# First projection of a hybrid layer in token layout, MoBA values 512 wide, and a new order of all engines

## The chip, the cores and the metric

The kernel runs on one core of a Trainium2 chip. The metric is the device time of one execution in microseconds; lower is better. The engines are named as the profile names them: PE is TensorE (matmuls; PEld its weight loads), DVE is VectorE, ACT is ScalarE, POOL is GpSimd, SP is SyncE, which issues the DMAs.

## The reference

One decoder layer on 256 tokens of width 1024, in fp32. One input projection gives the columns of three groups of heads, each group mixes the tokens in its own way and is multiplied by its own gate, and one output projection with a layer norm ends the layer:

```python
h = jnp.einsum('btd,de->bte', x, w_in)            # 256 x 1024 by 1024 x 4176
h_gla, h_moba, h_rwkv = _split(h, [GLA_COLS, MOBA_COLS, RWKV_COLS])
o = jnp.concatenate([_gla_branch(h_gla, ...), _moba_branch(h_moba, ...), _rwkv_branch(h_rwkv, ...)], axis=-1)
y = jnp.einsum('bte,ed->btd', o, w_out)
return _layer_norm(DN_ALPHA * x + y, ln_w, ln_b)
```

GLA (4 heads of 64) is linear attention with a decay for each channel, which comes from 16 low-rank columns. MoBA (8 heads) is causal softmax attention with a bias by relative position; at 256 tokens its one block is the whole sequence. RWKV-7 (4 heads) is a recurrence over the tokens whose state is multiplied by a diagonal and a rank-one term in each step; its decay and its in-context rate come from 64 low-rank columns.

## The kernel before

**Projections.** The columns of `w_in` are cut on the host into 16 units of 256 columns (`starts`, `wun`), and the 80 low-rank columns. x comes transposed, in 8 chunks of 128 input channels, with the columns of unit 0 and the low-rank columns beside it (`xw0`, DMA chunks `xw`). fp32 products are made of three fast matmuls: each operand is split into a high part (`hi`, a copy on ACT that rounds) and a low part (`lo`, a subtraction on DVE), and hi x hi, hi x lo and lo x hi are added up in PSUM (`terms`). So a unit costs a DMA of 1 MB into a `raw` tile, two `hi` copies on ACT, two `lo` subtractions on DVE (`prep`), and 48 matmuls of 256 columns on PE: 8 chunks x 3 terms x 2 halves. In channel layout (`proj_ch`) the weights are the stationary operand and x is streamed; in token layout (`proj_tok`) x is stationary and the weights are streamed. Groups of 6 matmuls (`GRAIN`) stay together.

**The first group** needs no `raw` tile, since its weights come with x: unit 0, the RWKV keys (`pk`, two PSUM tiles of 256 columns), and the low-rank columns (`pg`, 80 rows). For each chunk, ACT and DVE split x (256 columns), unit 0 (256) and the low-rank part (80); the first chunk is multiplied in plain fp32 without a split. Eight matmuls on a constant (`warm`) stand at its head.

**Mixers.** RWKV builds a 128 x 128 matrix `AT` for each pair of heads, solves triangular systems of 32 rows with DVE (`pre`, `T`, 31 steps), transposes the result (`TT`), and goes on from there through `pX`, `X`, `pP`, `U`, `M`, `yr` to `orw`. MoBA makes scores `pL` of heads 0 to 3 and 4 to 7 from split queries and keys, adds the bias `nB` and takes the row maximum in one DVE instruction for each piece (256 and 128 columns), and exponentiates on ACT (`L`), scales by `rc`, transposes (`pPm`, `PT`), and multiplies by the values `mv` (`pO`, `omb`). Each branch's output is split once more (`ohr`, `ohg`, `ohm`: high parts for RWKV, GLA and MoBA) for the output projection `yo`, whose weights (`rawo`) ACT centres and splits. PSUM has two pools of four banks, `pj` (projections, half of the scores, `yo`) and `sm` (the rest). SBUF tiles of the tag `big` (3 buffers) hold `AT`, `nB`, `xres` and `lwb` one after another.

**Order.** Every instruction is only recorded (`Plan`, `Proxy`); `emit`, whose line is L369 in the profile, then issues the 958 recorded operations in the order of the table `ORDER`, and each engine runs its own in that order. So the place of an instruction is a matter of the table, and all lines of the profile say L369; tiles tell the instructions apart.

## Time and profile before

| | us |
|---|---|
| median of 3 runs | 170.37 |
| lowest and highest | 168.59, 172.09 |
| the profiled execution | 168.87 |
| its span, first to last instruction | 167.2 |
| PE, DVE, ACT, POOL busy | 156.0, 143.1, 118.6, 29.1 |

The profiled execution's own time is 1.67 us longer than its span; the sum of the prediction is made against 168.87. Busy times overlap, since the engines run side by side; which of them decides changes along the span, and the views of the section below are cut by stretch for that reason.

### The profile page before, as it was taken

The page shows a single profiled execution, that of the slowest core. Times are in us where ns is not written, and L with a number is a line of the kernel's source. Part 1 is how long each engine was busy: PE and PEld are TensorE (multiplying, and loading weights), DVE is VectorE, ACT ScalarE, POOL GpSimd, SP SyncE. Part 2 cuts the span into 40 slices and gives each one's busy share as a digit, 9 for nine tenths or more (in the row PEclk, how much of TensorE's full clock was granted, in tenths as well). Part 3 has the DMA queues.
Part 4 walks back from the last instruction along what each step waited for, and adds up shares of the span by engine and source line. Part 5 has one row for each costly group of instructions (what it writes and reads, how often), then busy time and mean ns, then how long its engine had stood idle before and what let it go on. Part 6 is the DMA issues. An engine that isn't in the chain of part 4 may idle for free.

```text
span 167.2 us, 3968 instructions
## 1 busy us (share of the span) xinstructions
PE 156.0 (93%) x1507; PEld 144.6 (86%) x1507; DVE 143.1 (86%) x339; ACT 118.6 (71%) x270; POOL 29.1 (17%) x65
## 2 busy tenths in 40 slices
PE   8869999999999999999999998998998999999940
PEld 3659999999999999999999998997887977888940
DVE  0696899999899999899999999998964969886892
ACT  3494998979934486598683999969998979930000
POOL 8670008930000000001000000000003580120000
PEclk9999999999999999999999999999999999999995
DMA  5999285498466979772850745796243800000203
GB/s 147 328 363 340 105 277 228 129 360 287 114 216 181 167 269 301 281 257 54 253 195 4 250 145 146 208 328 226 70 185 107 258 18 0 0 0 0 94 36 126
DMA packets 18195, 29.47 MB, mean 176 GB/s; under 512 B 6472, under 2 KB 11040, under 8 KB 18176
## 3 DMA queue, kind: packets, MB, share of 16 engines
q1 hardware_dynamic: 18176, 29.21, 55.4%
q8 instruction: 12, 0.20, 0.4%
q14 instruction: 7, 0.06, 0.1%
HBM read 26.97 MB, written 2.24 MB: 175 GB/s over the span
## 4 chain that ended last, share of the span: by engine, by line
PE 42%; DVE 27%; ACT 11%; DMA 8%; issue 7%; SPq 2%; DVEq 0%; ACTq 0%
PE yo L369 13%; DVE lo L369 9%; DMA nB<-vd 5%; DVE pre L369 4%; PE pgq L369 4%; PE pgk L369 3%; PE pv L369 3%; PE pmk L369 3%; DVE L L369 3%; DMA xw<-in_xw_dram 3%; DVE T L369 3%; ACT rawo L369 3%; PE pmq L369 2%; PE pmg L369 2%; DVE Z L369 2%
## 5 line engine op out<-in xcount | busy, mean ns | idle before, releaser
L369 ACT ACTIVATE hi<-raw 128x1024 fp32r<-128x1024 f32 (+1 forms) x32 | 31.2, 998 | 15.0 <-PE pmv L369 3.1
L369 DVE TENSOR_TENSOR lo<-raw,hi 128x1024 fp32r<-128x1024 f32 (+1 forms) x32 | 36.7, 1158 | 0.6 <-ACT hi L369 0.5
L369 POOL TENSOR_SCALAR suo<-suo 128x1 f32<-128x1 f32 x8 | 2.6, 333 | 85.4 <-ACT rawo L369 85.3
L369 DVE SCALAR_TENSOR_TENSOR loo<-rawo,suo,hio 128x512 fp32r<-128x512 f32 (+1 forms) x12 | 10.9, 922 | 0.4 <-ACT hio L369 0.4
L369 DVE TENSOR_TENSOR pre<-T,A 128x1 f32<-128x1 f32 (+30 forms) x31 | 10.3, 331 | 0.5
L369 ACT ACTIVATE lsd<-lmv,eps 128x1 f32<-128x1 f32 x2 | 0.6, 294 | 13.9 <-DVE lmv L369 13.9
L369 ACT ACTIVATE hio<-rawo,suo 128x512 fp32r<-128x512 f32 (+1 forms) x12 | 9.9, 855 | 0.0
L369 PE MATMUL pmg<-xhi,hi 128*128 128x256 f32 x32 | 9.6, 300 | 0.0
L369 PE MATMUL pmv<-hi,xhi 128*128 128x256 f32 x32 | 9.6, 299 | 0.0
L369 PE MATMUL pmk<-xhi,hi 128*128 128x256 f32 x32 | 9.1, 285 | 0.0
L369 PE MATMUL pmq<-xhi,hi 128*128 128x256 f32 x32 | 9.1, 284 | 0.0
L369 PE MATMUL pmg<-xhi,lo 128*128 128x256 f32 x32 | 9.0, 282 | 0.0
L369 PE MATMUL pmg<-xlo,hi 128*128 128x256 f32 x32 | 9.0, 282 | 0.0
L369 PE MATMUL pmq<-xlo,hi 128*128 128x256 f32 x32 | 9.0, 282 | 0.0
L369 PE MATMUL pmq<-xhi,lo 128*128 128x256 f32 x32 | 9.0, 281 | 0.0
L369 PE MATMUL pmv<-lo,xhi 128*128 128x256 f32 x32 | 9.0, 281 | 0.0
L369 PE MATMUL pmv<-hi,xlo 128*128 128x256 f32 x32 | 9.0, 281 | 0.0
L369 PE MATMUL pmk<-xlo,hi 128*128 128x256 f32 x32 | 9.0, 281 | 0.0
L369 PE MATMUL pmk<-xhi,lo 128*128 128x256 f32 x32 | 9.0, 281 | 0.0
L369 ACT ACTIVATE rawo<-rawo 128x1024 f32<-128x1024 f32 x8 | 8.4, 1054 | 0.0
L369 DVE TENSOR_REDUCE T<-pre 128x1 f32<-128x2 f32 (+30 forms) x31 | 7.9, 254 | 0.4
L369 ACT ACTIVATE L<-L,mx 128x256 f32<-128x256 f32 (+1 forms) x16 | 7.1, 447 | 0.3 <-DVE mx L369 0.3
(352 smaller groups left out, 618.4 us busy)
## 6 DMA issues: line engine op xcount, KB each, us to landing
raw<-in_wun_dram SPq DMA_DIRECT2D x28, 512.0 KB, 4.8
rawo<-in_wo_dram SPq DMA_DIRECT2D x8, 512.0 KB, 4.8
xw<-in_xw_dram SPq DMA_DIRECT2D x8, 296.0 KB, 5.1
raw<-in_wun_dram SPq DMA_DIRECT2D x4, 256.0 KB, 6.0
nB<-vd SPq DMA_DIRECT2D x1, 1024.0 KB, 8.3
xres<-in_xr_dram SPq DMA_DIRECT2D x1, 1024.0 KB, 7.6
out_dram<-y SPq DMA_DIRECT2D x3, 256.0 KB, 2.1
dT<-AT SPq DMA_DIRECT2D x2, 256.0 KB, 6.7
```

Of the source, the lines that this page charges most:

```text
L369: self.tc.keep_in_program_order(fn(*args, **kw))
```

## The change

- **First group.** Unit 0 becomes the GLA values. They and the 80 low-rank columns are projected together in token layout, 336 columns wide, into two PSUM tiles `pgv` (one for each 128 tokens). The splits of unit 0 and of the low-rank part become one of 336 columns (`first`: six chunks in one `big` buffer for high and one for low parts, the last chunk in small tiles). ACT copies the low-rank columns to `g0`, PE transposes them back into channel layout (`pg`), and ACT copies the values to `gv`.
- **Units.** The RWKV keys are now unit 1 with a projection of their own (`kproj`, `pk`), RWKV r is unit 2 (one PSUM tile `pr`), and the RWKV values unit 6. The GLA value projection of before, and its ACT copy, are gone.
- **MoBA values.** Units 8 and 9 are laid out on the host as 4 chunks of 512 columns each, and one projection makes all 512 value columns: 48 matmuls of 512 in groups of 3, into `pmv0` and `pmv1`, which hold a PSUM bank each from the first group of three until four ACT copies of 256 columns.
- **Loads.** All eight x chunks are issued ahead of the parameters and the bias table.
- **Warm matmuls.** Eight as before; seven then one stood at the head of the first group, now two stand there, three within it, and three further on in the stream.
- **Order.** The table has 928 entries, in another order throughout. Among others, scores `pL` 4 to 7 come early as before, `pL` 0 to 3 behind the RWKV solve.

```diff
 KC = 8
 LEVELS = (4, 8, 16, 32)
 ORDER = (
...
-    950, 951, 956, 957, 952, 954, 953, 955)
+    903, 899, 897, 910, 908, 909, 911, 912, 916, 917, 900, 919, 898, 920, 918, 921, 922, 923, 924, 926, 925, 927)
...
-    gp = ctx.enter_context(tc.tile_pool(name="gp", bufs=35))
+    gp = ctx.enter_context(tc.tile_pool(name="gp", bufs=37))
...
-    hi0 = wp.tile([128, KC, T], F32R, tag="hi", name="hi0")
-    lo0 = wp.tile([128, KC, T], F32R, tag="lo", name="lo0")
-    units[0] = (hi0, lo0)
-    g0hi = cp.tile([128, KC, 80], F32R, name="g0hi")
-    g0lo = cp.tile([128, KC, 80], F32R, name="g0lo")
+    first = []
+    for nm in ("h", "l"):
+        most = gp.tile([128, 6, XW - T], F32R, tag="big", bufs=3, name=f"f{nm}")
+        rest = gt(f"f{nm}7", (128, XW - T), F32R)
+        first.append([None] + [most[:, k] for k in range(6)] + [rest])
     with plan.at(-2000):
         for k0, k1 in steps[1:] + steps[:1]:
             k = slice(k0, k1)
             raw = xw[k0 // 4][:, k0 % 4:k0 % 4 + k1 - k0]
             split(xhi[:, k], xlo[:, k], raw[:, :, 0:T])
             if k0:
-                split(hi0[:, k], lo0[:, k], raw[:, :, T:2 * T])
-                split(g0hi[:, k], g0lo[:, k], raw[:, :, 2 * T:XW])
+                split(first[0][k0], first[1][k0], raw[:, 0, T:XW])
...
-    def proj_tok(u, name):
-        p = pj(name)
-        for t in range(2):
-            for n, (k, x, w) in grains(terms(XS, units[u])):
-                PE.matmul(p[:, t * 256:(t + 1) * 256], lhsT=x[:, k, t * 128:(t + 1) * 128], rhs=w[:, k, :],
-                          start=(n == 0), stop=(n == 23))
-        return p
...
-    pk = [pj(f"pk{c}") for c in range(2)]
-    pg = pj("pg0")
+    pgv = [pj(f"pgv{t}") for t in range(2)]
     with plan.at(-1500):
-        for c in range(2):
-            PE.matmul(pk[c][:, 0:256], lhsT=xw[0][:, 0, T + c * 128:T + (c + 1) * 128], rhs=xw[0][:, 0, 0:T], start=True, stop=False)
-        PE.matmul(pg[:80, 0:256], lhsT=xw[0][:, 0, 2 * T:XW], rhs=xw[0][:, 0, 0:T], start=True, stop=False)
-        for n, ((k, w, x), (_, wg, _)) in enumerate(zip(terms(units[0], XS), terms((g0hi, g0lo), XS))):
+        for t in range(2):
+            PE.matmul(pgv[t][:, 0:XW - T], lhsT=xw[0][:, 0, t * 128:(t + 1) * 128], rhs=xw[0][:, 0, T:XW], start=True, stop=False)
+        for n, (k, x, w) in enumerate(terms(XS, first)):
             if k == 0:
                 continue
-            for c in range(2):
-                PE.matmul(pk[c][:, 0:256], lhsT=w[:, k, c * 128:(c + 1) * 128], rhs=x[:, k, :], start=False, stop=(n == 23))
-            PE.matmul(pg[:80, 0:256], lhsT=wg[:, k, :], rhs=x[:, k, :], start=False, stop=(n == 23))
+            for t in range(2):
+                PE.matmul(pgv[t][:, 0:XW - T], lhsT=x[:, k, t * 128:(t + 1) * 128], rhs=w[k], start=False, stop=(n == 23))
+    gv = cp.tile([128, 512], F32, name="gv")
+    g0 = gt("g0", (128, 160))
+    for t in range(2):
+        S.activation(g0[:, t * 80:(t + 1) * 80], pgv[t][:, 256:336], AF.Copy)
+    pg = sm("pg0", (128, 256))
+    transposes([(pg[:80, t * 128:(t + 1) * 128], g0[:, t * 80:(t + 1) * 80]) for t in range(2)])
+    for t in range(2):
+        S.activation(gv[:, t * 256:(t + 1) * 256], pgv[t][:, 0:256], AF.Copy)
+
+
+    plan.section = "kproj"
+    pk = [pj(f"pk{c}") for c in range(2)]
+    for n, (k, w, x) in grains(terms(units[1], XS)):
+        for c in range(2):
+            PE.matmul(pk[c][:, 0:256], lhsT=w[:, k, c * 128:(c + 1) * 128], rhs=x[:, k, :], start=(n == 0), stop=(n == 23))
...
-    pr = [pj("pr0"), sm("pr1")]
-    for n, (k, w, x) in grains(terms(units[1], XS)):
-        for c in range(2):
-            PE.matmul(pr[c][:, 0:256], lhsT=w[:, k, c * 128:(c + 1) * 128], rhs=x[:, k, :], start=(n == 0), stop=(n == 23))
-    rf = shift(pr, 0, "rf")
+    rf = shift(proj_ch(2, "pr"), 0, "rf")
     V.tensor_mul(ar[:, :, 1, :], rf.rearrange("p (a b) -> p a b", b=128), Pf[:, :, 1:129])
 
+    prep(6)
...
-    pv = proj_ch(2, "pv")
+    pv = proj_ch(6, "pv")
...
     prep(8)
+    prep(9)
...
+    def moba_values():
+
+        plan.section = "mv0"
+        ps_ = [pj(f"pmv{t}") for t in range(2)]
+        for q in range(2):
+            wh, wl = (w.rearrange("p (a b) c -> p a (b c)", b=2) for w in units[8 + q])
+            for t in range(2):
+                for k in range(4):
+                    with plan.group():
+                        for n, (x, w) in enumerate(((xhi, wh), (xhi, wl), (xlo, wh))):
+                            PE.matmul(ps_[t], lhsT=x[:, q * 4 + k, t * 128:(t + 1) * 128], rhs=w[:, k, :],
+                                      start=(q == 0 and k == 0 and n == 0), stop=(q == 1 and k == 3 and n == 2))
+        for i in range(2):
+            o = gt(f"mv{i}")
+            for t in range(2):
+                S.activation(o[:, t * 256:(t + 1) * 256], ps_[t][:, i * 256:(i + 1) * 256], AF.Copy)
+            mvt.append(o)
+
     def moba_proj(i):
-        for kind, u, dst in (("v", 8 + i, mvt), ("q", 10 + i, mq), ("k", 12 + i, mk)):
+        if i == 0:
+            moba_values()
+        yield
+        for kind, u, dst in (("q", 10 + i, mq), ("k", 12 + i, mk)):
             plan.section = f"m{kind}{i}"
-            p = proj_tok(u, f"pmv{i}") if kind == "v" else proj_ch(u, f"pm{kind}{i}")
-            if kind == "v":
-                o = gt(f"mv{i}")
-                S.activation(o, p, AF.Copy)
-            else:
-                c = 0.125 if kind == "q" else 1.0
-                hi, lo = gt(f"mh{kind}{i}", dt=F32R), gt(f"ml{kind}{i}", dt=F32R)
-                S.activation(hi, p, AF.Copy, scale=c)
-                V.scalar_tensor_tensor(lo, p, c, hi.bitcast(F32), op0=ALU.mult, op1=ALU.subtract)
-                o = (hi, lo)
-            dst.append(o)
+            p = proj_ch(u, f"pm{kind}{i}")
+            c = 0.125 if kind == "q" else 1.0
+            hi, lo = gt(f"mh{kind}{i}", dt=F32R), gt(f"ml{kind}{i}", dt=F32R)
+            S.activation(hi, p, AF.Copy, scale=c)
+            V.scalar_tensor_tensor(lo, p, c, hi.bitcast(F32), op0=ALU.mult, op1=ALU.subtract)
+            dst.append((hi, lo))
...
-    prep(6)
     next(it)
-    prep(9)
...
-    plan.section = "gv"
-    pvg = proj_tok(6, "pgv")
-    gv = gt("gv")
-    S.activation(gv, pvg, AF.Copy)
...
-    starts = [RW + 256, RW, RW + 512, RW + 768, GL, GL + 256, GL + 512, GL + 768]
+    starts = [GL + 512, RW + 256, RW, RW + 768, GL, GL + 256, RW + 512, GL + 768]
     starts += [MB + 1024, MB + 1280, MB, MB + 256, MB + 512, MB + 768, MB + 1536, MB + 1792]
+    wide = cols(MB + 1024, 512).reshape(128, 2, KC, 256)
+    units = [wide[:, i - 8] if i in (8, 9) else cols(c, 256) for i, c in enumerate(starts)]
...
-        wun=np.stack([cols(s, 256) for s in starts]),
+        wun=np.stack(units),
```

The order moves nearly everything; three places follow. Names are tiles, output left of the arrow, and the numbers are buffer numbers.

PE at its start, before (`xw` is the unsplit first chunk, `xhi` and `xlo` the split x, `hi0` and `g0hi` the split first weights):

```order
L369 MATMUL warm_74<-const-bfloat16-1.0 128x512
L369 MATMUL pk0_105<-xw0_72 128x256
L369 MATMUL pk1_106<-xw0_72 128x256
L369 LDWEIGHTS const-bfloat16-1.0
L369 MATMUL warm_74<-const-bfloat16-1.0 128x512
L369 MATMUL pg0_107<-xw0_72 80x256
L369 MATMUL pg0_107<-xhi_80,g0hi_84 80x256
L369 MATMUL pk1_106<-xhi_80,hi0_82 128x256
L369 MATMUL pk0_105<-xhi_80,hi0_82 128x256
L369 MATMUL pg0_107<-xlo_81,g0hi_84 80x256
L369 MATMUL pg0_107<-xhi_80,g0lo_85 80x256
```

PE at its start, after (`fh` and `fl` are the split first weights of 336 columns):

```order
L367 MATMUL warm_74<-const-bfloat16-1.0 128x512
L367 MATMUL pgv1_106<-xw0_72 128x336
L367 LDWEIGHTS const-bfloat16-1.0
L367 MATMUL warm_74<-const-bfloat16-1.0 128x512
L367 MATMUL pgv0_105<-xw0_72 128x336
L367 MATMUL pgv0_105<-fh_82,xhi_80 128x336
L367 MATMUL pgv0_105<-fl_84,xhi_80 128x336
L367 MATMUL pgv0_105<-fh_82,xlo_81 128x336
L367 MATMUL pgv1_106<-fh_82,xhi_80 128x336
L367 MATMUL pgv1_106<-fl_84,xhi_80 128x336
L367 MATMUL pgv1_106<-fh_82,xlo_81 128x336
```

Three matmuls for each term, with the low-rank ones 80 rows high, become two of 336 columns; of the warm matmuls all but a few are gone from the head.

PE around the scores of heads 4 to 7 (`pL4` to `pL7`), before (`pmk0` is the projection of MoBA keys):

```order
L369 MATMUL pmv0_257<-hi8_217,xhi_80 128x256
L369 MATMUL pmv0_257<-lo8_218,xhi_80 128x256
L369 MATMUL pmv0_257<-hi8_217,xlo_81 128x256
...
L369 MATMUL pL6_344<-mlk1_338,mhq1_331 128x128
L369 MATMUL pL7_345<-mlk1_338,mhq1_331 128x128
L369 MATMUL pmk0_268<-xhi_80,hi12_260 128x256
L369 MATMUL pmk0_268<-xlo_81,hi12_260 128x256
L369 MATMUL pmk0_268<-xhi_80,lo12_261 128x256
```

The same place after (`pv` is the projection of RWKV values):

```order
L367 MATMUL pL6_345<-mlk1_339,mhq1_332 128x128
L367 MATMUL pL7_346<-mlk1_339,mhq1_332 128x128
L367 MATMUL pmv0_266<-hi8_223,xhi_80 128x512
L367 MATMUL pmv0_266<-lo8_224,xhi_80 128x512
L367 MATMUL pmv0_266<-hi8_223,xlo_81 128x512
...
L367 MATMUL pmv1_267<-lo8_224,xhi_80 128x512
L367 MATMUL pmv1_267<-hi8_223,xlo_81 128x512
L367 MATMUL pv_168<-xhi_80,hi6_145 128x256
L367 MATMUL pv_168<-xlo_81,hi6_145 128x256
L367 MATMUL pv_168<-xhi_80,lo6_146 128x256
```

Ahead of the scores one value projection of 48 matmuls was finished, with one PSUM tile; after, 15 of the 512-wide matmuls follow the scores and two value tiles stay open, and the next projection behind them is `pv`.

ACT from the first copy behind the solve (`X`), before:

```order
L369 ACTIVATE gr_373<-pgr_372,der_99 128x256
L369 ACTIVATE L5_352<-L5_352,rc5_355 128x256
L369 ACTIVATE X_177<-pX_178 32x8x32 x2
L369 ACTIVATE PT6_363<-pPm6_362 128x384
L369 ACTIVATE rawo3_394,suo30_397<-rawo3_394 128x1024
L369 ACTIVATE TT_102<-pP_179 32x8x32 x2
L369 ACTIVATE PT4_351<-pPm4_350 128x384
L369 ACTIVATE St1_227<-pS641_236 64x2x64 x2
L369 ACTIVATE X_177<-pX64_180 64x4x64 x2
L369 ACTIVATE rawo3_394,suo31_398<-rawo3_394 128x1024
```

ACT from the same copy, after (`L0` to `L3` with `sm` are the exponentials, `hi14` the high part of a MoBA gate unit):

```order
L367 ACTIVATE X_183<-pX_184 32x8x32 x2
...
L367 ACTIVATE hi14_378<-raw14_377 128x1024
L367 ACTIVATE TT_102<-pP_185 32x8x32 x2
L367 ACTIVATE gate_rt_375<-gr_374 128x512
...
L367 ACTIVATE L0_283,sm0_285<-L0_283,mx0_284 128x256
...
L367 ACTIVATE L2_295,sm2_297<-L2_295,mx2_296 128x128
...
L367 ACTIVATE L0_283,sm0_285<-L0_283,mx0_284 128x128
...
L367 ACTIVATE L1_289,sm1_291<-L1_289,mx1_290 128x256
...
L367 ACTIVATE L1_289,sm1_291<-L1_289,mx1_290 128x128
```

Ahead of X all sixteen exponentials had been done; after, the eight of heads 0 to 3, and the split of `hi14`, follow X.

## Rows read from the trace of the kernel before

**Rows 1.** The page: busy time and slices of TensorE, and the chain by engine.
```profile
PE 156.0 (93%) x1507; PEld 144.6 (86%) x1507; DVE 143.1 (86%) x339; ACT 118.6 (71%) x270; POOL 29.1 (17%) x65
...
PE   8869999999999999999999998998998999999940
...
PE 42%; DVE 27%; ACT 11%; DMA 8%; issue 7%; SPq 2%; DVEq 0%; ACTq 0%
```

**Rows 2.** The chain that ended last, pieces: start us, length us, what.
```profile
27.64 1.42 PE pgk L369 x12
...
138.47 22.35 PE yo L369 x120
```

**Rows 3.** Busy time by stretch: PE, PEld, DVE, ACT, POOL (instructions), clock, DMA, GB/s.
```profile
15.00:20.00 5.00, 5.00 (x44) 5.00 (x43) 2.84 (x6) 3.87 (x9) 0.00 (x0) 1.00 0.60 219
115.00:120.00 5.00, 4.88 (x90) 4.35 (x92) 5.00 (x11) 4.84 (x12) 0.25 (x2) 1.00 0.15 56
125.00:130.00 5.00, 4.37 (x63) 4.06 (x63) 2.61 (x10) 4.36 (x11) 1.28 (x2) 1.00 0.39 103
20.00:110.00 90.00, 89.37 (x902) 87.82 (x900) 87.26 (x210) 71.13 (x150) 9.99 (x19) 1.00 0.68 204
110.90:147.20 36.30, 34.99 (x391) 30.34 (x392) 28.87 (x68) 33.73 (x84) 8.57 (x16) 1.00 0.36 121
```

**Rows 4.** What TensorE waited for: us in total, times, longest.
```profile
PE pk L369 <- DVE xlo L369: 1.5, 1, 1.5
```

**Rows 5.** Timeline, 0 to 12 us, all engines: start, length, what, [idle before].
```profile
0.83 3.15 PE L369 MATMUL warm<-const-bfloat16-1.0 128*128 128x512 bf16 x7 [0.83 <-PEq L1372]
...
3.80 2.08 PE L369 MATMUL pk<-xw 128*128 128x256 f32 x4
...
8.55 2.54 DVE L369 TENSOR_SCALAR der<-prm 128x1 f32<-128x1 f32 x4
...
8.86 2.23 DVE L369 TENSOR_TENSOR xlo<-xw,xhi 128x256 fp32r<-128x256 f32 x1
...
9.26 1.79 POOL L369 MEMSET AT<- 128x2048 f32 x1
...
11.16 0.50 PE L369 MATMUL pk<-xlo,hi 128*128 128x256 f32 x2 [1.52 <-DVE xlo L369]
```

**Rows 6.** Timeline of TensorE at three places.
```profile
16.35 0.40 PE L369 MATMUL pr<-xhi,hi 128*128 128x256 f32 x2
...
148.17 0.39 PE L369 MATMUL yo<-hio,ohm 128*128 128x512 f32 x1
148.40 0.39 PE L369 MATMUL yo<-loo,ohm 128*128 128x512 f32 x1
```

**Rows 7.** VectorE instructions that read the score tile pL.
```profile
L369 DVE CUSTOM_DVE_ANT_0 L<-nB,pL x16: 274/346/422, 71.4 to 102.5; 128x256 f32<-128x256 f32 x8, 128x128 f32<-128x128 f32 x8
```

**Rows 8.** Timeline of VectorE: the second transpose of the solve.
```profile
109.18 0.57 DVE L369 STREAM_TRANSPOSE TT<-TT 96x384 f32<-96x384 f32 x1
```

**Rows 9.** Timeline of ScalarE behind the solve, first and last instruction used.
```profile
110.89 0.78 ACT L369 ACTIVATE X<-pX 32x256 f32<-32x256 f32 x2 [1.33 <-PE pX L369]
...
145.44 1.14 ACT L369 ACTIVATE ohm<-omb 128x512 fp32r<-128x512 f32 x2
```

**Rows 10.** ScalarE by kind: busy us, mean ns of one.
```profile
L369 ACT ACTIVATE hi<-raw 128x1024 fp32r<-128x1024 f32 x28 | 28.8, 1052 | 15.0 <-PE pmv L369 3.1 <-PE pgq L369 2.9 <-PE pgg L369 2.9
...
L369 ACT ACTIVATE L<-L,mx 128x256 f32<-128x256 f32 x8 | 4.0, 504 | 0.3 <-DVE mx L369 0.3
...
L369 ACT ACTIVATE L<-L,mx 128x128 f32<-128x128 f32 x8 | 3.1, 390 | 0.0
...
L369 ACT ACTIVATE L<-L,rc 128x256 f32<-128x256 f32 x4 | 2.0, 502 | 0.0
...
L369 ACT ACTIVATE mv<-pmv 128x512 f32<-128x512 f32 x2 | 1.2, 590 | 0.0
...
L369 ACT ACTIVATE W<-pW 128x256 f32<-128x256 f32 x2 | 0.7, 360 | 0.0
```

82 rows, old and new, of the table ORDER are left out of this document.

## The prediction

> **What bounds the kernel now.** I read the page first [rows 1]. TensorE is busy 156.0 of 167.2 us, and in the slices its only clearly lower ones are the first two, the stretch past the middle and the last. So work taken off TensorE counts wherever nothing else ends later, and the question is where that is. The chain that ended last [rows 2] finishes with 22.35 us of `yo` matmuls, from 138.47 to about 160.8; behind them come 6.4 us of VectorE and output DMA up to the span's end, which the change leaves as they are.
>
> The stretches [rows 3] tell the rest. From 20 to 110 us TensorE is busy 89.4 of 90 and VectorE 87.3: two engines are full side by side, ScalarE (71.1) is not. From 110.9 to 147.2 it is ScalarE that is nearly full, 33.7 of 36.3, and in the middle of it (115 to 120) 4.84 of 5. That stretch begins with the first copy `X` behind the solve (110.89), and ends with the two splits `ohm` of the attention output (145.44 + 1.14 = 146.58) [rows 9]. The `yo` matmul on `ohm` at 148.17 [rows 6] is the seventh of its run, so the first, six steps of 0.23 earlier, starts at 146.8: barely after its operand. So the chain is: start, then VectorE and TensorE together until the solve, then ScalarE until `ohm`, then fixed work: some 14 us of TensorE and the 6.4.
>
> **The start.** Before, 63 matmuls of 256 columns (3 for each term) and 3 fp32 ones make the first group; the next projection starts at 16.35 [rows 6]. In it TensorE waits 1.5 us for one `xlo` split [rows 4]. The cause stands in the timeline [rows 5]: a VectorE instruction on `der` that starts at 8.55 and the splits queued behind it end only at about 11.1, when the GpSimd memset of `AT` (9.26, 1.79 long) ends; the matmul follows at 11.16. After, 42 matmuls of 336. A stream of 256-wide ones runs at 1.42/12 = 0.118 us each [rows 2], two 512-wide ones start 0.23 apart [rows 6]; a straight line gives 0.153 for 336 (an estimate). So 63 x 0.118 = 7.5 becomes 42 x 0.153 = 6.4 us: **-1.1**. ScalarE and VectorE each do 7 splits of 336 in place of 7 of 256 and 7 of 80, which is less, and `der` and the second memset of `AT` now stand behind the splits (the memset waits for tiles of the first group). So the wait of 1.5 should go, at most **-1.5**. Against it: the clock. Before, seven warm matmuls run from 0.83 to 3.98, 0.45 each, twice the later pace, that is at the lower of the two levels (1.2 and 2.4 GHz), and the two pairs of fp32 records that follow also take long (2.08 us) [rows 5]. After only two stand ahead, so TensorE sits idle before the first chunk and the full rate may come later. Each 336-wide matmul at half rate costs 0.153 more; six to twelve of them are 0.9 to 1.8. Sum: between +0.3 and -2.6; I take **-1.5**, since the stall of 1.5 has a visible cause that is moved.
>
> The rule that bears on these widths is in the Trainium skill, "TensorE: Matmul & The Clock Gate", section "Back-to-back issue gap": a warm matmul takes columns/2.4 plus about 2.5 ns. By it 256 columns cost 109 ns and 512 cost 216; the trace has 118 and about 230, so here a matmul carries about 12 ns that don't shrink, and wide ones save a little more than the page says. By the page the first group would lose 63 x 109 - 42 x 142.5 = 0.9 us, not 1.1.
>
> **The middle.** The RWKV key projection becomes a normal one, 48 matmuls of 256 (48 x 0.118 = +5.7), and the later GLA value projection of the same size goes (-5.7): nothing. The MoBA values: 96 x 0.118 = 11.3 become 48 x 0.23 = 11.0, **-0.3**; up to -1.3 if the gaps at changes of operand are also saved, but groups of three, strewn among other work, keep these. Two transposes of the low-rank columns and three warm matmuls in the full stream (0.23 each) add **+0.9**. So from the first group on TensorE has about +0.6 (-0.4 to +0.7) and everything that it gains it gains at the start. ScalarE copies of `g0` and `gv` (4, some 0.3 each) fall into 15 to 20 us, where it was busy 3.87 of 5 and VectorE 2.84 [rows 3]; nothing there is late.
>
> **The solve comes earlier.** VectorE was full from 20 to 110, so what stands ahead of the second transpose of the solve (109.18 [rows 8]) sets when `X` can start. Before, all 16 reads of `pL` are done by 102.5 [rows 7]; after, the 8 of heads 0 to 3 stand behind the transposes: 4 x 0.42 + 4 x 0.27 = 2.8 us. With 1.5 from the start, X moves from 110.9 to about 110.9 - 2.8 - 1.5 = 106.6, perhaps 105 if more of VectorE's queue went back.
>
> **The tail pays for it.** What was put behind X on ScalarE, by its rows [rows 10]: 8 exponentials (4 x 0.504 + 4 x 0.390 = 3.6), two weight splits `hi14` (2.1, which stood ahead), two more scalings of `L` (1.0), four copies of 256 columns (W's price, 4 x 0.36) in place of one of 512 (0.59), +0.85. That is 7.5; each starts some 0.1 before its predecessor ends, and three small `St` copies go, so about **+6.0**. ScalarE had 36.3 - 33.7 = 2.6 us of idle time there. If it fills half of it, X to `ohm` takes 35.7 + 6.0 - 1.3 = 40.4, so `ohm` ends at 106.6 + 40.4 = 147.0 with the late X, 145.4 with the early one. Before: 146.58. So between +0.4 and -1.2; with 2.6 filled -2.5, with none +1.7. I take **-0.9**, near the early X, because the three terms that set it (start, `pL` reads, `der`) all point that way.
>
> **Forecast.** The profiled execution took 168.87 us for a span of 167.2. -0.9 gives 168.0. The median of the runs shown is 170.37 (168.59 to 172.09), and the median of these three and the profiled one 169.6, so the profiled one is 0.4% under the middle; as a timed median I say 168.87 - 0.9 + 0.75 = **168.7**. About 2% (3.4 us) is what a measurement of this kernel can tell from no change.
>
> **Rivals.** *TensorE's work decides, not ScalarE's.* If the strewn order hides the extra 6 us (TensorE idles 0.12 us from 115 to 120 and 0.63 from 125 to 130 [rows 3]; such gaps are what an order can fill), then the start gives its full -2.6, gaps like those two between 100 and 130 some -1.5 (an estimate: twice the two), and the middle -0.4: -4.5, so 164.4 profiled, 165.1 timed. For it: ScalarE stood at 71.1 of 90 ahead of the solve, so it has room to run ahead. Against: the exponentials can't be ahead, since their scores are behind X. Chance 0.18.
>
> *Two PSUM banks are held* (slower). `pj` has four banks. `pmv0` and `pmv1` now hold two from the end of `pmq1` until the copies far in the tail; before, one projection held one bank for its 5.7 us and a copy. With two left, `pL6` and `pL7` take both, and `pv` can start only when VectorE has read one of them. Only 15 matmuls of 512 lie between, 15 x 0.23 = 3.5 us. Before, the 16 reads of `pL` lie strewn from 71.4 to 102.5 [rows 7], one in every 2 us of VectorE's full queue; at that pace the three reads that free `pL7` (its two, and one of `pL6` between) take 4 to 6 us. TensorE then stops for 1 to 2 us at `pv`, and the same can come again at each later projection that has two banks. With 4.5 us of such stops and no gain from the start, 168.87 + 4.5 - 0.5 = 172.9, 173.6 timed: slower by over 2%. It decides from about 4 us on; below that it only eats the gain. Chance 0.14.
>
> *The start doesn't gain* (clock late, and `AT`'s memset meets `der` again some 4 us later): X at 108, 147.0 + 1.5 for `ohm`, 168.87 + 1.9 = 170.8, 171.5 timed. Within 2%. Chance 0.18. My forecast with its neighbours has the remaining 0.50.
>
> **Range and chances.** Forecast with its own bounds: 168.7 (167.0 to 171.2). The case of the full gain reaches to 165.1, the held banks to 173.6; leaving out half of each gives **165.2 to 172.0**. Faster by over 2%: 0.18; slower by over 2%: 0.14; within: 0.68.
>
> **What would show it.** In the changed profile: the first group ends before 15 us and TensorE no longer waits for `xlo`; the middle is still full on TensorE and VectorE; X starts between 105 and 107; ScalarE is full from there to `ohm`, which ends near 146; `yo`, the last TensorE piece, ends around 160. Wrong, if TensorE waits at `pv` or a later projection for more than 1 us (banks), if the first group runs at the lower clock for several us, or if `ohm` is ready long before `yo` asks for it, in which case TensorE's sum decides and the time falls further.

## The result, and the profile after

The changed kernel takes 169.69 us (median of 4 runs, 169.11 to 170.0) beside 169.48 for the kernel before in the same four rounds (166.79 to 172.09); the ratio of the two is 1.0136, with a 95% interval of 1.0091 to 1.0181. The ratio is taken over runs in the faster of two states that executions show, and two of the four of the kernel before (170.37 and 172.09) were in the slower one. So it is slower by 1.4%, some 2.3 us, where 1.7 us faster than the median shown, or about 0.9 us faster than the profiled run, was forecast. With more runs of the kernel before (25, 24 and 35 in three later sessions) its median is 167.71, 168.15 and 167.91: the three runs shown ahead had a median of 170.37, and the profiled one took 168.87, which is 1.0 more than this kernel mostly takes. So part of the loss lies in what the change was measured against, and no profile here shows the kernel before in an execution as fast as its median.

The page of the changed kernel: busy times, slices of TensorE and its clock, and the chain by engine.

```profile
PE 155.5 (93%) x1438; PEld 141.6 (84%) x1438; DVE 142.3 (85%) x332; ACT 119.1 (71%) x268; POOL 27.5 (16%) x65
...
PE   3999999979999999999999999989999999899940
...
PEclk9999999999999999999999999999999999999998
...
DVE 38%; PE 19%; ACT 15%; issue 11%; DMA 8%; POOL 5%; SPq 2%; POOLq 1%; DVEq 0%; ACTq 0%
```

TensorE does 0.5 us less than before [rows 1], and idles 12.5 instead of 11.2 us of a span of 168.0 instead of 167.2. The chain that ended last has changed its owner: TensorE's share falls from 42% to 19%, VectorE leads, and GpSimd, which had no share before, has 5%.

The start: timeline of TensorE, start us, length us, what, [idle before].

```profile
0.83 1.01 PE L367 MATMUL warm<-const-bfloat16-1.0 128*128 128x512 bf16 x2 [0.83 <-PEq L1383]
3.75 1.49 PE L367 MATMUL pgv<-xw 128*128 128x336 f32 x2 [1.91 <-DMA xw<-in_xw_dram]
...
7.70 0.48 PE L367 MATMUL pgv<-fl,xhi 128*128 128x336 f32 x1
7.98 0.48 PE L367 MATMUL pgv<-fh,xlo 128*128 128x336 f32 x1
...
9.57 0.32 PE L367 MATMUL pgv<-fl,xhi 128*128 128x336 f32 x1
9.72 0.31 PE L367 MATMUL pgv<-fh,xlo 128*128 128x336 f32 x1
...
14.79 0.39 PE L367 MATMUL pk<-xhi,hi 128*128 128x256 f32 x2
```

The first group ends at 14.79, 1.56 earlier than in [rows 6], and no `xlo` is waited for. But the matmuls of 336 columns start 0.28 us apart until 9.38 and 0.155 apart from there: about twelve of them ((9.38 - 6.08) / 0.28; some records are missing) ran at the lower of the two clock levels. This is read from the pace; the clock row of the page shows 9 there too.

The way from there to `kkt` (the RWKV keys' step ahead of the solve), VectorE and GpSimd:

```profile
29.42 0.35 POOL L367 TENSOR_SCALAR ss<-ss 128x8 f32<-128x8 f32 x1 [12.36 <-DVE ss L367]
29.71 1.28 POOL L367 COPY vec<-tb 8x27 f32<-8x27 f32 x1
29.72 2.36 DVE L367 TENSOR_TENSOR lo<-raw,hi 128x1024 fp32r<-128x1024 f32 x2
30.96 2.64 POOL L367 TENSOR_TENSOR rs<-ss,mhalf 128x8 f32<-128x8 f32 x1
33.64 0.69 DVE L367 TENSOR_TENSOR kkt<-pkk,rs 128x512 f32<-128x512 f32 x1 [1.56 <-POOL rs L367]
60.64 0.15 DVE L367 TENSOR_TENSOR pre<-T,A 128x1 f32<-128x1 f32 x1
```

`kkt` waits 1.56 us for GpSimd's `rs`, in front of which a copy of `vec` stands. The last row is the first step of the solve, at 60.64. In the profile before it starts at 60.65, so all that the start had gained was gone by then:

```profile
60.65 0.15 DVE L369 TENSOR_TENSOR pre<-T,A 128x1 f32<-128x1 f32 x1
```

In three later profiles of the same start (the kernel before once more and with two small edits, below) it starts at 58.78 to 59.01.

Behind the solve: ScalarE's `X` and the splits `ohm`, TensorE's last run of `yo` (from the chain), and two waits of TensorE (us in total, times, longest).

```profile
107.16 0.78 ACT L367 ACTIVATE X<-pX 32x256 f32<-32x256 f32 x2 [0.72 <-PE pX L367]
...
145.02 0.62 ACT L367 ACTIVATE ohm<-omb 128x512 fp32r<-128x512 f32 x1
...
148.07 0.64 ACT L367 ACTIVATE ohm<-omb 128x512 fp32r<-128x512 f32 x1 [1.82 <-DVE omb L367]
...
144.30 17.41 PE yo L367 x95
...
PE pkn L367 <- DVE kkt L367: 1.2, 1, 1.2
...
PE yo L367 <- DVE loo L367: 0.5, 1, 0.5
```

`X` comes 3.73 us earlier than in [rows 9], and the `yo` matmuls end at 144.30 + 17.41 = 161.71, 0.89 later than in [rows 2] (138.47 + 22.35 = 160.82). What ends last ahead of them is no longer `ohm` but `loo`, the low part of an output weight, by way of ScalarE and GpSimd; that costs a stop of 0.5. Busy time by stretch (same columns as in [rows 3]):

```profile
14.79:107.16 92.37, 90.60 (x932) 86.56 (x931) 87.18 (x199) 69.00 (x142) 12.30 (x32) 1.00 0.64 202
107.16:161.71 54.55, 52.86 (x458) 45.34 (x458) 43.16 (x106) 40.46 (x105) 8.29 (x16) 1.00 0.32 107
117.00:145.60 28.60, 27.95 (x237) 24.37 (x238) 21.35 (x56) 28.04 (x80) 8.08 (x16) 1.00 0.47 161
```

The last row is the stretch to look at: from 117.0 to 145.6 ScalarE is busy 28.04 of 28.60 us, with one gap of 0.47 (for GpSimd's `suo`). Before, the tail from X took 160.82 - 110.89 = 49.93; now 54.55. The kernel before, by the same columns, from X on and from the last stop of TensorE on:

```profile
110.89:160.82 49.93, 48.60 (x467) 42.15 (x467) 39.62 (x86) 34.71 (x85) 9.76 (x17) 1.00 0.29 99
128.78:160.82 32.04, 32.02 (x208) 27.59 (x208) 26.17 (x51) 17.43 (x44) 8.03 (x12) 1.00 0.20 61
```

So before, TensorE was full for the last 32 us; its operand `ohm` came in time and did not hold it. From X on, ScalarE has 5.75 us more work than before, and TensorE 4.26 more.

### The profile page after: what moved, and what is told of

Read it like the earlier page. It is cut to its first block, busy times and chain, and to the rows that moved or that the text cites. A ratio compares the mean times of both kernels' runs of the same rounds, so it can differ in the third digit from the quotient of the medians.

```text
span 168.0 us, 3806 instructions
## 1 busy us (share of the span) xinstructions
PE 155.5 (93%) x1438; PEld 141.6 (84%) x1438; DVE 142.3 (85%) x332; ACT 119.1 (71%) x268; POOL 27.5 (16%) x65
## 4 chain that ended last, share of the span: by engine, by line
DVE 38%; PE 19%; ACT 15%; issue 11%; DMA 8%; POOL 5%; SPq 2%; POOLq 1%; DVEq 0%; ACTq 0%
DVE lo L367 11%; PE yo L367 10%; DMA raw<-in_wun_dram 8%; DVE pre L367 5%; DVE T L367 4%; PE pgq L367 3%; PE pmq L367 3%; ACT L L367 3%; SPq L367 2%; DVE Z L367 2%; ACT rawo L367 2%; PE pA L367 2%; POOL rs L367 2%; ACT hi L367 1%; DVE d L367 1%
## 5 line engine op out<-in xcount | busy, mean ns | idle before, releaser
L367 ACT ACTIVATE hi<-raw 128x1024 fp32r<-128x1024 f32 (+1 forms) x32 | 31.7, 1003 | 12.5 <-issue 3.5
L367 DVE TENSOR_TENSOR lo<-raw,hi 128x1024 fp32r<-128x1024 f32 (+1 forms) x32 | 37.6, 1184 | 0.9 <-ACT hi L367 0.9
L367 POOL TENSOR_SCALAR suo<-suo 128x1 f32<-128x1 f32 x8 | 3.3, 418 | 87.5 <-ACT rawo L367 87.5
L367 ACT ACTIVATE hio<-rawo,suo 128x512 fp32r<-128x512 f32 (+1 forms) x12 | 10.5, 887 | 0.5 <-POOL suo L367 0.5
L367 DVE TENSOR_TENSOR fl<-xw,fh 128x336 fp32r<-128x336 f32 x7 | 3.3, 504 | 5.0 <-ACT fh L367 5.0
L367 PE MATMUL pmv<-hi,xhi 128*128 128x512 f32 x16 | 7.2, 453 | 0.0
L367 PE MATMUL yo<-loo,ohm 128*128 128x512 f32 (+1 forms) x20 | 6.9, 347 | 0.0
```

Of the source, the lines that this page charges most:

```text
L367: self.tc.keep_in_program_order(fn(*args, **kw))
```

## The experiments

The medians are device times. The runs of one session share their runs of the kernel before; its medians are given above, in the order of the sessions. The changed kernel itself was run again only in the first one, so what the later ones are set beside, 169.7 and after's profile, comes from other sessions.

### First session: where the time goes ahead of the solve

**The same kernel once more** (no edit), to see how far two profiles of one kernel agree.

> The changed kernel as it is, on the chip that the next three also run on: the measure for them. Both theories expect the ratio to the kernel before that was measured first, 1.009 to 1.018, and X near 107.2 us, the second ohm near 148.1.

169.68 us, ratio 1.0131 (1.0020 to 1.0242). Span 167.9. The loss repeats, at the same size, with a wide interval.

**`rs` ahead of the copy on GpSimd.** Each number is an operation's place in the record; 195 is `rs`, 552 the copy of `vec`.

```diff
+def moved(order, *steps):
+    order = list(order)
+    for op, ahead_of in steps:
+        order.remove(op)
+        order.insert(order.index(ahead_of), op)
+    return tuple(order)
+ORDER = moved(ORDER, (195, 552))
```

> The changed kernel with one GpSimd instruction moved: rs stands ahead of the copy into vec that stood between ss and rs. Theory 1 (each engine's queue passes a shift on to the end: what is won ahead of the solve is won at the end, and the tail only adds its own length): DVE's wait of 1.56 us for rs falls to about 0.3 and TensorE's of 1.16 us goes, X starts 1.0 to 1.3 us earlier (106.0) and the execution is 1.0 to 1.3 us shorter. Theory 2 (the tail is full on ScalarE whatever comes ahead of it, and other waits take the place): X moves, the end by less than 0.4 us.

168.27 us, ratio 1.0050 (0.9998 to 1.0102): 1.4 less than the unchanged kernel in the same session. Its timeline:

```profile
29.74 2.60 POOL L376 TENSOR_TENSOR rs<-ss,mhalf 128x8 f32<-128x8 f32 x1
32.31 0.20 POOL L376 COPY vec<-tb 8x27 f32<-8x27 f32 x1
...
32.38 0.69 DVE L376 TENSOR_TENSOR kkt<-pkk,rs 128x512 f32<-128x512 f32 x1 [0.43 <-POOL rs L376]
...
59.24 0.17 DVE L376 TENSOR_TENSOR pre<-T,A 128x1 f32<-128x1 f32 x1
```

`kkt` waits 0.43 instead of 1.56, TensorE's wait for it is gone, and everything behind comes some 1.4 earlier: the solve from 59.24, `X` at 105.78, the 95 `yo` from 142.89. From `X` to these `yo` it is 37.11 us, as after (37.14). So in the changed kernel time saved ahead of the solve reaches the end whole.

**Seven warm matmuls at the head again** (operations 10 to 15), as before, in place of two.

```diff
+ORDER = moved(ORDER, (10, 96), (11, 96), (12, 96), (13, 96), (14, 96), (15, 95))
```

> The changed kernel with its eight warm matmuls where the kernel before has them: seven at the head, one between the first two fp32 matmuls, none later. The first group runs at the full rate from the start of its split terms and ends 1.3 to 2.0 us earlier (13 us in place of 14.8), and 0.7 us of TensorE work leaves the stream. Theory 1: X and the end come 1.0 to 2.0 us earlier. Theory 2: the first group ends earlier, and the key chain behind it (ss, rs, kkt) waits for something else; the end moves by less than 0.4 us.

168.26 us, ratio 1.0057 (1.0024 to 1.0090): 1.4 less. The timeline of TensorE shows why:

```profile
0.83 3.15 PE L376 MATMUL warm<-const-bfloat16-1.0 128*128 128x512 bf16 x7 [0.83 <-PEq L1392]
...
6.14 0.31 PE L376 MATMUL pgv<-fl,xhi 128*128 128x336 f32 x1
6.29 0.32 PE L376 MATMUL pgv<-fh,xlo 128*128 128x336 f32 x1
...
13.47 0.40 PE L376 MATMUL pk<-xhi,hi 128*128 128x256 f32 x2
```

The pace is 0.155 from 6.14 on, the second matmul of the first split chunk, and the first group ends at 13.47. So the two warm matmuls at the head, with 1.9 us of idle time behind them, are what made the clock late; the prediction had named this against itself.

**Three scalings of `L` on VectorE**, to take 1.2 us (3 x 0.40, start to start) off ScalarE in the tail.

```diff
-                if h:
+                if h and head == 5:
                     S.activation(L[:, 0:256], L[:, 0:256], AF.Copy, scale=rc[:, 0:1])
                 else:
                     V.tensor_scalar_mul(L[:, 0:256], L[:, 0:256], rc[:, 0:1])
```

> The changed kernel with three scalings of the probabilities (heads 1, 3 and 7, behind the solve) on VectorE in place of ScalarE: 1.2 us less on ScalarE between X and ohm, 1.0 us more on VectorE, which has room from 115 to 120 us. If ScalarE's sum sets the tail: the second ohm and the end come 0.8 to 1.2 us earlier. If TensorE's work or the chain through VectorE sets it: no change, or up to 0.5 us later.

168.82 us, ratio 1.0081 (1.0040 to 1.0122): 0.9 less by the medians. In the profile the way from `X` (106.46) to the 95 `yo` (143.18) is 36.72 us, only 0.42 less than after's 37.14: ScalarE caught up and then waited for TensorE, whose `pmv` was not done:

```profile
127.96 0.38 ACT L367 ACTIVATE mv<-pmv 128x256 f32<-128x256 f32 x1 [0.37 <-PE pmv L367]
```

In that execution `X` also came 0.70 earlier than in after's profile, 0.42 of it at the start (its first group ended at 14.37), which the edit does not touch. So the run shows that ScalarE is on the path, and that TensorE stands close behind it: of 1.2 us a third comes back.

### Second session: which engine sets the tail

**Less TensorE work in the tail.**

```diff
+ORDER = tuple(i for i in ORDER if i not in (796, 799))
```

> After, but two of the groups of matmuls of pmg0 are left out (part of the MoBA gate projection is not computed): 12 matmuls of 256 columns at 0.119, 1.43 us less TensorE work between X and the end, none of it on ScalarE or VectorE. Theory 3, TensorE's work and idle time set the end, and ScalarE's tail follows it: the yo run starts about 1.4 earlier, 169.7 becomes 168.3. Theory 4 (the prediction's chain: ScalarE from X to ohm sets the end): ohm stays near 148, yo waits for it, 169.4 to 169.7, with TensorE's new idle time seen as a wait for ScalarE or VectorE.

169.13 us, ratio 1.0086 (1.0055 to 1.0117). `X` at 106.46, the 95 `yo` from 143.60: 37.14 us, to the hundredth what after has. 1.43 us of TensorE's work in the tail (the groups that went stood behind 128 us) are worth nothing. The execution profiled took 169.05, 0.73 less than after's, and had that gain at its start already (first group done at 13.93, `X` 0.70 earlier). The expectation from TensorE's sum falls, for work that stands behind 128 us.

**More ScalarE work in the tail.**

```diff
+    spare = cp.tile([128, 32], F32, name="spare")
+    with plan.group():
+        for _ in range(8):
+            S.activation(spare, ones[:, 0:32], AF.Copy)
     plan.emit()
...
+ORDER = moved(ORDER + (928,), (928, 853))
```

> After, with eight spare copies of 128x32 on ScalarE (some 0.2 each, 1.6 us together) ahead of a hio split near 129 us; what they write nobody reads. Theory 4 (ScalarE from X to ohm sets the end): ohm, and with it yo, some 1.6 later, 169.7 becomes 171.3. Theory 3 (TensorE's sum): ScalarE has little room there, but TensorE has work queued ahead of what waits for it, so between 0 and +0.8: 169.7 to 170.5.

171.18 us, ratio 1.0202 (1.0155 to 1.0249): 1.5 more than after by the medians, 0.7% by the ratios. The chain's last `yo`, and the spare copies in the timeline of ScalarE:

```profile
129.06 2.12 ACT L376 ACTIVATE spare<-ones 128x32 f32<-128x32 f32 x8
...
145.22 17.41 PE yo L376 x95
```

They took 2.04 us (129.06 to the next instruction at 131.10), and with `X` at 106.13 the way to `yo` is 39.09: 1.95 longer. Nearly every tenth that ScalarE gets more at 129 us is paid at the end. Together with the run before it: from there on the changed kernel is bound by ScalarE.

**MoBA values 256 wide again.**

```diff
-                            PE.matmul(ps_[t], lhsT=x[:, q * 4 + k, t * 128:(t + 1) * 128], rhs=w[:, k, :],
-                                      start=(q == 0 and k == 0 and n == 0), stop=(q == 1 and k == 3 and n == 2))
+                            for c in (0, 256):
+                                PE.matmul(ps_[t][:, c:c + 256], lhsT=x[:, q * 4 + k, t * 128:(t + 1) * 128], rhs=w[:, k, c:c + 256],
+                                          start=(q == 0 and k == 0 and n == 0 and c == 0), stop=(q == 1 and k == 3 and n == 2 and c == 256),
+                                          skip_group_check=True)
```

> After, with the MoBA values' 48 matmuls of 512 columns cut into 96 of 256 (the same sums in the same place of the order). The prediction priced the width at -0.3 us (96 x 0.118 against 48 x 0.23), so this run should lose that again: +0.3 to +0.5 ahead of X, 170.1. If the wide form itself had cost something (a slower 512-wide matmul), it comes out faster than 169.7.

169.18 us, ratio 1.0103 (1.0051 to 1.0155); not told apart from after, and by the medians 0.5 faster, not slower as expected. The profile doesn't show the price of the width either. From the first group's end to `X` it takes 106.58 - 13.75 = 92.83, 0.46 more than after, but this lies ahead of the solve, where no value matmul stands yet: from the solve's first step (60.06) to `X`, where more than half of them stand (28 of after's 48, 55 of 96 here), it is 46.52 in both. Behind `X` it takes 37.95 to the `yo`, 0.8 more. There ScalarE waits for a late `pM`, and the stretches show why (same columns as above; the clock is the third number from the end):

```profile
118.27 0.31 ACT L367 ACTIVATE M<-pM,dM 64x64 f32<-64x64 f32 x1 [0.52 <-PE pM L367]
...
108.00:112.00 4.00, 3.23 (x54) 2.81 (x47) 3.38 (x18) 3.87 (x8) 0.00 (x0) 1.00 0.44 131
112.00:116.00 4.00, 4.00 (x33) 3.93 (x33) 4.00 (x12) 3.91 (x12) 0.00 (x0) 0.59 0.17 22
```

From 112 to 116 TensorE was granted 0.59 of its clock; after has 1.00 there. This execution was also the longest of the six (170.59; the others 169.00 to 169.90). So neither a loss nor a gain of the wide form is shown. What the run does show, unplanned, is that some 1.6 us less of TensorE's full pace (4 x 0.41, an estimate) at 112 to 116 us goes with an end 0.8 later.

**The three edits of the first session together.**

> After with all three edits that helped alone: rs ahead of the vec copy on GpSimd (-1.4), warm matmuls at the head (-1.4), three scalings of L on VectorE (-0.9). If they add, as they must if each takes away its own idle time of TensorE: 169.7 - 3.7 = 166.0, X at about 104.3. If two of them use the same slack: 167 to 168.

166.93 us, ratio 0.9953 (0.9917 to 0.9989). `X` at 104.19, the 95 `yo` from 140.91: it does what the sum of the parts said for X (104.3), and the median is 0.9 above the 166.0 expected. It is the fastest version here, 2.8 us below after. Against the kernel before it stands 0.5% better, which is as much as the unchanged kernel before differs from itself in the next session.

### Third session: the kernel before again

**Before, unchanged.**

> Before, unchanged, for a second profile of it. The first one (168.87) lies above the 167.7 and 168.15 that its other runs have as median. If the first was only a slow one at the start, X comes near 110.0 here and the span near 166.2; if it is typical, X is at 110.9 again. The ratio should hold 1.

168.70 us, ratio 1.0045 (1.0005 to 1.0086), so half a per cent is not told here even where an interval leaves out 1. Of its profile only the part up to `X` is used, since behind it TensorE's clock fell (0.63 granted from 116 to 124, below), which the first profile of this kernel doesn't show. Start and `AT` memset:

```profile
8.28 0.52 DVE L369 TENSOR_SCALAR der<-prm 128x1 f32<-128x1 f32 x4
...
10.25 1.80 POOL L369 MEMSET AT<- 128x2048 f32 x1
...
11.34 0.74 DVE L369 TENSOR_SCALAR der<-prm 128x2 f32<-128x2 f32 x1
...
14.60 0.40 PE L369 MATMUL pr<-xhi,hi 128*128 128x256 f32 x2
...
58.91 0.15 DVE L369 TENSOR_TENSOR pre<-T,A 128x1 f32<-128x1 f32 x1
...
109.27 0.77 ACT L369 ACTIVATE X<-pX 32x256 f32<-32x256 f32 x2 [1.39 <-PE pX L369]
```

This is the run that settles the start. The same program, and no TensorE wait for `xlo`: the four `der` of [rows 5] were done when the memset began (here 1 us later), one later `der` took 0.74, and the first group ended at 14.60, not 16.35. The solve starts at 58.91, and `X` comes at 109.27 (expected near 110.0 or 110.9).

**`AT`'s second memset out of the way, in before** (operation 108 behind the first one).

```diff
+ORDER = moved(ORDER, (108, 91))
```

> Before, with GpSimd's memset of AT1 moved ahead of the masks, right behind that of AT0, so that it no longer meets der on VectorE. Prediction: the stall of der and TensorE's wait of 1.5 for xlo go, the first group ends 1.5 earlier, and since the way from there to the end is full, the end comes 1.5 earlier: 168.0 becomes 166.5. Rival: the start's gain is spent before the solve (as in after, where the solve starts at 60.6 in both kernels): 168.0, with X where it was.

168.42 us, ratio 1.0027 (0.9994 to 1.0061): no gain. Its first group ended at 14.47, 0.1 to 0.2 ahead of `b_again` (14.60) and the run below (14.71). Of the expected 1.5 nothing comes, since neither of those two, with the memset where it was, had the stall. (Both memsets of `AT` now meet an earlier `der`, of 128x9, which took 2.99 us instead of 1.27; TensorE did not wait for it.)

**A copy of `vec` between `ss` and `rs`, in before.**

```diff
+ORDER = moved(ORDER, (564, 222))
```

> Before, with one copy of vec (8x37) on GpSimd put between ss and rs, as a copy of vec stands there in after. If that detour is on the path between the first group and the solve, kkt, the solve and the end come 1.0 to 2.0 later (the copy, and rs longer by up to 0.9): 169.0 to 170.0. If before has other work for VectorE and TensorE there, 168.0 to 168.3.

168.43 us, ratio 1.0013 (0.9978 to 1.0047). The copy took 0.43 there and `rs` 2.14, so the detour was smaller than in after, and `kkt` didn't wait:

```profile
24.31 0.43 POOL L378 COPY vec<-tb 8x37 f32<-8x37 f32 x1
24.71 2.14 POOL L378 TENSOR_TENSOR rs<-ss,mhalf 128x8 f32<-128x8 f32 x1
...
28.60 0.68 DVE L378 TENSOR_TENSOR kkt<-pkk,rs 128x512 f32<-128x512 f32 x1
```

Here `rs` is done at 26.85 and used at 28.60; the new order uses it as soon as it comes. Busy time from `X` to the end of `yo` in this run, which serves as a second profile of before's tail:

```profile
109.87:160.73 50.86, 48.54 (x467) 42.11 (x467) 39.74 (x86) 34.70 (x85) 9.75 (x17) 1.00 0.28 99
```

**After with both engines relieved**: `scale_dve` and `pe_less` in one.

> After with both relieved behind X: three scalings of L on VectorE as in the run scale_dve, and two groups of pmg0 left out as in pe_less (part of the MoBA gate projection is not computed). From X to the run of 95 yo after has 37.1 us, scale_dve 36.7, pe_less 37.1. If ScalarE is the first limit there and TensorE the next one, the two together give more than their sum: about 36.2 (another 0.4 to 0.6, TensorE's waited-for pmv and pPm come earlier). If something else stands behind ScalarE (VectorE, GpSimd's suo), 36.7 again.

168.73 us, ratio 1.0064 (1.0035 to 1.0094). From `X` (106.12) to the 95 `yo` (142.69) 36.57 us: 0.15 less than `scale_dve`, not 0.5. ScalarE waits for the same `pmv` by the same 0.37 as there, because both groups that were left out stand behind it: as many `pmg` matmuls (12) run ahead of the last `pmv` as in after. The run was aimed past its mark, and what follows ScalarE as the limit stays open.

## Why the prediction was wrong

By its own sum: start -1.5, the solve's queue -2.8, tail +4.7 (40.4 - 35.7), which is +0.4 against the profiled execution with the late X (106.6). It then took -0.9, "near the early X, because the three terms that set it (start, `pL` reads, `der`) all point that way". **This is the step that failed: X came at 107.16, later than the late one.** Two terms kept it from coming early: the late clock in the first group (without it, in `warm_head`, X comes at 105.52), which the prediction had set against a gain that it took in full, and a wait of 1.56 us for GpSimd's `rs`, which it had put at nothing (without it, in `rs_first`, 105.78). And the start's -1.5, which stands in both cases, rests on a stall that other executions of the kernel before don't have. The profiles, stage by stage (us; the end of the first group, from there to the solve's first step, from there to `X`, from there to the end of `yo`):

| | first group | to the solve | solve to X | X to end of yo | sum |
|---|---|---|---|---|---|
| before, profile shown | 16.35 | 44.30 | 50.24 | 49.93 | 160.82 |
| before, second profile | 14.60 | 44.31 | 50.36 | (clock fell) | |
| before with the `vec` copy | 14.71 | 44.30 | 50.86 | 50.86 | 160.73 |
| before with the memset moved | 14.47 | 44.31 | 50.32 | 50.97 | 160.07 |
| after | 14.79 | 45.85 | 46.52 | 54.55 | 161.71 |
| after, second profile | 14.71 | 45.61 | 46.50 | 54.77 | 161.59 |
| after, `rs_first` | 14.94 | 44.30 | 46.54 | 54.52 | 160.30 |
| after, `warm_head` | 13.47 | 45.53 | 46.52 | 54.50 | 160.02 |

**The start: wrong, though the number came out.** -1.5 "since the stall of 1.5 has a visible cause that is moved". Against the profile shown it is -1.56, as if right. But the stall belonged to that one execution: three other profiles of the same start have 14.47 to 14.71. Against these after's own two profiles, 14.71 and 14.79, gain nothing. Even the agreement with the shown profile is chance, since the parts differ: 42 wider matmuls in place of 63 save about 1 (63 x 0.118 is 7.4, not the 7.5 of the prediction, against 42 x 0.155 = 6.5, and `warm_head` ends 1.0 to 1.2 ahead of the undisturbed starts), and the late clock takes 12 x 0.125 = 1.5, of which `warm_head` gives back 1.3. The upper bound of the range (+0.3) had allowed for the late clock; the value was chosen from a row that doesn't repeat. One of the prediction's own signs of being wrong, the first group at the lower clock for several us, came true (6.08 to 9.38). How late the clock rises is itself uneven: eight executions of kernels with after's head end the first group between 13.75 and 14.94, the middle at 14.2, so the fair gain is some 0.4.

**To the solve: a wait that the prediction put at nothing.** All four profiles of before have 44.30 or 44.31 here. After has 45.85 and 45.61, and 44.30 again with `rs` in front of the copy (`rs_first`). So the detour on GpSimd costs 1.3 to 1.6 in these two. The prediction costed the order's moves on TensorE, VectorE and ScalarE and did not follow GpSimd's queue past `ss` and `rs`.

**Solve to X: right in direction, larger than forecast.** -2.8 was predicted for the eight reads of `pL` that go behind the solve; measured is -3.7 (46.52 against 50.24). Busy time in this stretch, before and after (same columns as in [rows 3]):

```profile
60.65:110.89 50.24, 49.71 (x577) 48.72 (x576) 48.20 (x151) 39.40 (x95) 0.92 (x3) 1.00 0.61 194
60.64:107.16 46.52, 45.98 (x543) 42.93 (x542) 45.62 (x133) 34.31 (x79) 1.59 (x4) 1.00 0.61 200
```

VectorE has 2.6 us less work there, near the 2.8, and 1.1 less idle time, which the prediction did not count. Together with the detour ahead of the solve, the way from the first group to `X` is 2.2 shorter.

**The tail: the size came out, the mechanism in part.** ScalarE's +6.0 less half of its idle time gave +4.7; X to the end of `yo` grew by 4.62 against the profile shown, 3.6 to 3.7 against the two other profiles of before that can be used, whose tails are 0.9 to 1.0 longer at the same busy time of ScalarE. ScalarE's busy time in that stretch grew by 40.46 - 34.71 = 5.75. That ScalarE's work sets the end of the changed kernel is shown behind 128 us: 2.0 us more on ScalarE cost 1.95, 1.43 less on TensorE nothing. But TensorE is close behind: 1.2 less on ScalarE gave back 0.42 only, and TensorE's work from X on grew by 4.26 as well. And the prediction's reading of the kernel before, ScalarE until `ohm`, was not what set its end: there TensorE ran full from 128.78 on, and `ohm` came 0.2 ahead of its use by the prediction's own rows (146.58 and 146.8). After, the end hangs on `hio` and `loo`; the second `ohm` is done at 148.71, past the forecast 146 to 147, and TensorE doesn't wait for it.

**A term left out.** The prediction gave TensorE's middle +0.6 and then did not put it into the sum; with it the sum is +1.0, beside +0.9 measured between the two profiled executions. This agreement is no proof either, since the terms of the way to X were off by more than that, in both directions.

**What stays open.** Against the profile shown, the miss of 1.8 us (+0.9 in place of -0.9) is nearly all the choice of the early X, 1.3, and the way to X, 0.6 (-2.2 in place of -2.8). Against the median of before the loss is 2.3 (1.0136 x 167.9 - 167.9). Of the rest no profile shows where it lies: the `yo` end 0.8 to 1.6 earlier in before's three complete profiles than in after's two, and the executions of these three took 168.12 to 168.87. The stall at the start is not it: without the stall X came 1.0 to 1.8 earlier in before, and the end only 0.1 to 0.75. In the run with the memset moved the chain goes there through the DMA of an output weight (`rawo`, 105.05 to 114.59); what a faster execution does in that place was not profiled.

**The rivals.** TensorE's sum alone does not decide in the tail of the changed kernel, at least not what stands behind 128 us (`pe_less`); earlier in the tail it may count (the slow stretch of `mv256`), which no run tested by itself. Up to the end of `yo` TensorE has 0.5 us less work than before and 1.4 more idle time (6.2 in place of 4.8), 1.2 of it the wait for `kkt`. Held PSUM banks did not stop TensorE at `pv` or a later projection: its longest waits are 1.9 for the first DMA and 1.2 for `kkt`. That held banks `pmv0` and `pmv1` are why the scores of heads 0 to 3 had to go behind `X`, and with them ScalarE's load, is argued from the order and was not tried. The third, the start that doesn't gain with a late clock, was the nearest: it put the end 1.9 us later, beside 0.9 against the profiled execution and 2.3 by the ratio. Its late clock is what `warm_head` shows; its other half, `der` meeting the memset of `AT` again, happened too (below) and cost TensorE nothing.

## What to carry to other kernels

A stall that stands in one profile is worth its price only if a second profile of the same program has it; where two engines meet by chance at a start, take a second one first, before a term is built on it. When a new order is costed, follow the small engines' queues between a producer and its waiter as closely as the large ones': a copy that takes 0.2 us elsewhere cost 1.4 at the end. Work moved behind the last serial stage, on an engine that then runs without a gap to the end, is paid nearly in full there (1.95 of 2.04). Time saved ahead of that stage reached the end whole in the changed kernel, whose tail takes the same from X on, and mostly not in the kernel before. And when a sum has an early and a late case, the sign of the forecast should not hang on the choice between them.

## What the runs showed of the hardware

**GpSimd beside VectorE.** The same `rs` (128x8) took 1.76 in before, 2.14 in `b_vec`, 2.60 in `rs_first` and 2.64 in after; a `vec` copy took 1.28 beside a `lo` subtraction (two `lo` from 29.72, 1.18 each) and 0.20 when it came later. The Trainium skill, "SBUF — State Buffer", section "SBUF: two separate sides", says that a VectorE instruction with two SBUF inputs and a GpSimd instruction that reads SBUF exclude each other for a whole instruction. The copy agrees: it ends at 30.99, about where the first `lo` ends (30.90). The rows of `rs` agree in direction only, since no run varied what stood beside it alone. With a GpSimd memset it was VectorE that took longer: the four `der` of before, 2.54 us in one execution with the `AT` memset in their midst, took 0.52 in the second profile, where the memset began after them. In after the same two meet once more, 4 us later:

```profile
13.71 1.82 POOL L367 MEMSET AT<- 128x2048 f32 x1 [1.74 <-PE pgv L367]
13.72 1.84 DVE L367 TENSOR_SCALAR der<-prm 128x4 f32<-128x4 f32 x1
...
14.39 1.17 DVE L367 TENSOR_SCALAR der<-prm 128x2 f32<-128x2 f32 x1
```

Both small instructions end with the memset, at 15.53 to 15.56; without a memset beside it the one of 128x2 took 0.16 in before. TensorE had its operands by then.

**The clock, at the start and in mid-kernel.** With a gap of 1.9 us behind two warm matmuls the lower level lasted to 9.38 in after, and with seven it was over at 6.14 (`warm_head`). Matmuls of 336 columns are 0.28 apart at the lower level and 0.155 at the upper one. The Trainium skill, "TensorE: Matmul & The Clock Gate", section "Back-to-back issue gap", gives columns/1.2 and columns/2.4 plus 2.5 ns for a single matmul, that is 0.280 and 0.1425 us: the first agrees, the second is 12 ns short, as for the widths in the prediction. And in the second profile of before the clock fell in mid-kernel, behind a stretch (112 to 116) in which TensorE was busy 3.05 of 4 us:

```profile
116.00:124.00 8.00, 7.54 (x63) 6.85 (x62) 4.19 (x9) 6.07 (x17) 0.56 (x2) 0.63 0.41 132
```

Nothing in the first profile of the same program hinted at it; the stretch is the one right behind the solve, where the RWKV steps leave TensorE gaps. In `mv256` it fell too, to 0.59 from 112 to 116, behind a stretch busy 3.23 of 4 us; with the memset moved TensorE was busy 3.02 of 4 us from 112 to 116, and the clock held.
